# Attention in a two-block transformer kernel: probabilities times V for two blocks of queries in one pass

## The chip, the cores and the metric

The kernel runs on one core of a Trainium2 chip. The metric is device time of one execution in microseconds (us); before the change three runs gave a median of 1279.34 us (1277.62 to 1280.61). A difference of about 0.2% (2.6 us) is what a measurement of this kernel can tell from no change.

## What is computed

512 tokens of width 1024 pass through two blocks. The first holds two attentions of eight heads each (one latent, "MLA", with a causal mask by chunks of 64, one over a band of chunks with a table of relative biases), gates, a routed mixture of 32 experts and norms. The second holds an attention of 16 heads over three dilations (in the kernel one causal attention whose mask carries the three dilations) beside a state-space scan, and a layer norm. What the change touches is the same in all three attentions, cut to its core:

```python
sc = jnp.einsum('bqhd,bkhd->bhqk', qb, k).astype(jnp.float32) * scale
sc = jnp.where(mask[None, None], sc, NEG_INF)
p = jax.nn.softmax(sc, axis=-1).astype(v.dtype)
return jnp.einsum('bhqk,bkhd->bqhd', p, v)
```

## The kernel before, in words

All of this is one program whose order is written out by hand: each engine executes its instructions in the order in which the Python code issues them. TensorE works off two kinds of work, woven into each other: the attention's own short steps, and "fillers", long dense products (projections, 24 matmuls of 512 columns each per job) that stand in a queue of generators. `fill(ns)` issues fillers worth about so many nanoseconds of matmul; a debt is carried over, and a filler is issued in steps of 640 ns (three matmuls), 853 ns or 430 ns. When a filler job ends, it issues its evacuation (`fin_conv`, `scaled`, `fin_z`, `keep`, `fin_rope` and others) on VectorE and ScalarE; when the next one starts, its weights are split into a high and a low part (`whalf`: ScalarE writes `whi`, line 223, VectorE `wlo`, line 224).

`attention(units, filler, first)` (line 658) is called twice: for the first block with 32 units and 1700 ns of filler per step, for the second with 32 units and 5400 ns. A unit is one block of 128 queries (`i` from 0 to 3) of a pair of heads (`s` is 0 or 1); four units make a pair of heads, and block `i` sees keys 0 to 128(i+1). Step `idx` of the loop issues, in this order:

- the scores of unit `idx` into PSUM tiles `ps_sc` (line 680, or lines 235 to 237 as three products of split operands), then on VectorE the biased scores with their minimum (`st`, `mn`, line 683) and on ScalarE the exponentials with their sums (`p`, line 691);
- `fill(filler)`;
- the transposes of the probabilities of unit `idx-1` into `ps_tr` (line 703), and their copies into the tiles `pt`: of head 0 on ScalarE (line 708), of head 1 on VectorE (line 706);
- on VectorE, the division of unit `idx`'s probabilities by their sums (lines 715 and 716);
- the products with V for unit `idx-2` into `ps_o` (line 722): a product is 64 output rows by 128 queries, two heads side by side in the array, one such pair of products per block of keys. TensorE's trace shows two instructions for each 32-bit product and transpose, so 10 pairs of products of a pair of heads are 40 instructions.

So a unit's copies have a whole further step of filler before the products read them, and a unit's division has a step's filler before its transposes read it. The loop runs two steps past the last unit. `ps_o` has one buffer, `ps_sc` and `ps_tr` two, the tiles `pt` four.

Of the kernel before, what the change touches and what calls it, by code (L numbers as in the profile page):

```python
# [13 lines left out]
AF = mybir.ActivationFunctionType  # L14
# [4 lines left out]
P = 128  # L19
# [49 lines left out]
def tile_block(ctx: ExitStack, tc: tile.TileContext, xT, cols_d, rows_d, ln_d, consts_d, tabs_d, positions,  # L69
               w_ada, w1, v1, w_uq, w_ukv, rel, w_o, w_out, w_r, w_e, w2, v2, w_out2, out):  # L70
    nc = tc.nc
    pe, ve, se, ge = nc.tensor, nc.vector, nc.scalar, nc.gpsimd
# [9 lines left out]
    def big(name, dt=F32):  # L82
        return ap.tile([P, 512], dt, tag="a", name=name)
# [3 lines left out]
    def tmp(name, dt=F32):  # L87
        return tp.tile([P, 512], dt, tag=name, name=name, bufs=TEMPS[name])
# [3 lines left out]
    def bank(tag, dt=F32):  # L92
        return pp.tile([P, 512], dt, tag=tag, name="ps_" + tag, bufs=BANKS[tag])
# [60 lines left out]
    def step():  # L154

        if running[0] is None:
            if not queue:
                return 0
            job = queue.pop(0)
            job.start()  # L160
            if not job.wide:
                ahead()
            flush()
            running[0] = (job, job.gen())
        job, g = running[0]
        c = next(g, None)
        if c is None:
            job.done = True
            running[0] = None
            return 1  # L170
        return c
# [3 lines left out]
    def fill(ns):  # L175
        debt[0] += ns
        while debt[0] > 0:
            c = step()
            if c == 0:
                debt[0] = 0.0  # L180
                return
            debt[0] -= c
# [468 lines left out]
    for t in range(4):  # L651
        o = bank("d")
        sl = slice(t * P, (t + 1) * P)
        mm3(o, kv_h[0][:, sl], kv_l[0][:, sl], wv[0], wv[1], True, True)
        v = big("va")
# [2 lines left out]

    def attention(units, filler, first):
        n = len(units)  # L660
        for idx in range(n + 2):
            if idx < n:
                u = units[idx]
                for nxt in units[idx:idx + 2]:
                    nxt["need"]()
                if not idx:
                    fill(first)
                u["before"]()
                qs, ks, rsl, tab, scale = u["qk"]()
                i = u["i"]  # L670
                w = P * (i + 1)
                u["st"], u["mn"] = [], []
                for s in range(2):
                    sc = bank("sc")
                    sl = slice(i * P, (i + 1) * P)
                    if isinstance(qs[s], tuple):
                        (qh, ql), (kh, kl), wide = qs[s], ks[s], max(w, 256)
                        mm3(sc[:, :wide], qh[rsl[s], sl], ql[rsl[s], sl], kh[rsl[s], :wide], kl[rsl[s], :wide], True, True)
                    else:
                        pe.matmul(sc[:, :w], qs[s][rsl[s], sl], ks[s][rsl[s], :w], start=True, stop=True)  # L680
                    st = tmp("st")
                    mn = small([P, 1], "mn")
                    ve.tensor_tensor_reduce(st[:, :w], sc[:, :w], tab[s][:, 512 - w:], op0=OP.add, op1=OP.min,  # L683
                                            scale=-scale, scalar=3e38, accum_out=mn)
                    u["st"].append(st)
                    u["mn"].append(mn)
                u["p"], u["l"] = [], []
                for s in range(2):
                    pt = tmp("p")
                    l = small([P, 1], "l")  # L690
                    se.activation(pt[:, :w], u["st"][s][:, :w], AF.Exp, bias=u["mn"][s], scale=-1.0, accum_out=l)  # L691
                    u["p"].append(pt)
                    u["l"].append(l)
                u["mid"]()
            fill(filler)
            if 0 <= idx - 1 < n:
                u = units[idx - 1]
                w = P * (u["i"] + 1)
                u["t"] = []
                for s in range(2):  # L700
                    tr = bank("tr")
                    for j in range(u["i"] + 1):
                        pe.transpose(tr[:, j * P:(j + 1) * P], u["p"][s][:, j * P:(j + 1) * P], ident)  # L703
                    tt = tmp("pt")
                    if s:
                        ve.tensor_copy(tt[:, :w], tr[:, :w])
                    else:
                        se.activation(tt[:, :w], tr[:, :w], AF.Copy)
                    u["t"].append(tt)
            if idx < n:  # L710
                u = units[idx]
                w = P * (u["i"] + 1)
                for s in range(2):
                    rl = small([P, 1], "rl")
                    ve.reciprocal(rl, u["l"][s])
                    ve.tensor_scalar(u["p"][s][:, :w], u["p"][s][:, :w], rl, None, op0=OP.mult)  # L716
            if 0 <= idx - 2 < n:
                u = units[idx - 2]
                i, o, v, vc = u["i"], u["o"](), u["v"], u["vc"]
                for j in range(i + 1):  # L720
                    for s in range(2):
                        pe.matmul(o[64 * s:64 * s + 64, i * P:(i + 1) * P], v(j)[:, vc + 64 * s:vc + 64 * s + 64],
                                  u["t"][s][:, j * P:(j + 1) * P], start=j == 0, stop=j == i,
                                  tile_position=(0, 64 * s))
                u["after"](o)
                for key in ("st", "p", "t"):
                    u.pop(key)

    def pair_units(jobs, before, qk, v, vc, fin):
        o = {}  # L730
# [56 lines left out]
    units = []  # L787
# [47 lines left out]
    x1, xr, u = [], [], []  # L835
# [17 lines left out]
    st = {}  # L853
# [49 lines left out]
    for m in range(KC):  # L903
        t = big("x1")
# [51 lines left out]
    u = None  # L956
# [75 lines left out]
    for t in range(5):  # L1032
        ts_ = range(4) if t == 4 else range(t + 1)
        for t2 in ts_:
            pe.matmul(rk[:, t * NE:(t + 1) * NE], trib if t2 == t else oneb, Ab[:, t2, :], start=t2 == 0,
                      stop=t2 == ts_[-1])
# [185 lines left out]
    o = bank("tr")  # L1222
# [102 lines left out]
    for gi, group in enumerate(GROUPS):  # L1325
# [5 lines left out]
        for b, n in enumerate(group):  # L1331
# [31 lines left out]
            pt, csh = slots_back([w[:, b * P:(b + 1) * P] for w in pw])  # L1363
# [18 lines left out]
    for m in range(8):  # L1382
        o = opened[m] if m < len(opened) else combine_open(outs[:-1], pts[:-1], m)
# [25 lines left out]
    with tc.For_i(0, nblk, 1):  # L1409
# [5 lines left out]
        for i in range(6):  # L1415
            for h in range(2):
                t = big("wo")
# [6 lines left out]
        for t in range(4):  # L1424
            s = slice(t * CAP, (t + 1) * CAP)
            ve.tensor_scalar(po_[:, s], iota, kb_[:, t:t + 1], None, op0=OP.is_equal)
            ve.tensor_scalar(pw_[:, s], po_[:, s].bitcast(F32), wb_[:, t:t + 1], None, op0=OP.mult)
        o = bank("d")
        for d in range(KC):
            for t in range(4):  # L1430
                g = 2 * t + d // 4
                s = slice((d % 4) * P, (d % 4 + 1) * P)
# [6 lines left out]
        o = bank("tr")  # L1439
        for t in range(4):  # L1440
            pe.transpose(o[:CAP, t * P:(t + 1) * P], pw_[:, t * CAP:(t + 1) * CAP], ident)
        pt, cs, junk = big("pt_", F32R), small([P, 1], "cs"), tmp("st")
# [5 lines left out]
        for k in range(KC):  # L1448
            pe.matmul(gu[:CAP], xo[:, k * CAP:(k + 1) * CAP], we[k],
                      start=k == 0, stop=k == KC - 1, tile_position=(0, 0))  # L1450
# [3 lines left out]
        for h in range(2):  # L1454
            o = bank("sc")
            for q in range(2):
                pe.matmul(o[:CAP], ht[:, q * P:q * P + CAP], we[8 + 2 * q + h], start=q == 0,
                          stop=q == 1, tile_position=(0, 0))
# [8 lines left out]
    o = bank("o")  # L1467
    for k in range(KC):
        j = k % 4
# [3 lines left out]
    for k in range(KC):  # L1473
# [8 lines left out]
        else:  # L1482
            t = tmp("sq")
# [233 lines left out]
    units = []  # L1717
    for p in range(NP):
        us = pair_units(lambda p=p: [jq[p], jk[p]], lambda p=p: load_tab(p), lambda p=p: ([q2[p]] * 2, [k2_[p]] * 2, half, tab2[p], 0.125),
                        lambda j, p=p: vt[4 * (p // 4) + j], (p % 4) * P, fin_att(p))  # L1720
# [148 lines left out]
    for t in range(4):  # L1869
        n = 1 if t < 3 else 2  # L1870
        for i in range(n):
            o = bank(("sc", "sc", "tr", "o")[t] if not i else "d")
            c = slice(i * 512 // n, (i + 1) * 512 // n)
# [7 lines left out]
        v, rr = small([P, 1], "lnv"), small([P, 1], "lnr")  # L1881
        ve.tensor_scalar(v, mv[:, 1:2], 1e-5, None, op0=OP.add)
        ge.tensor_tensor(rr, v, mhalf[:, 0:1], op=OP.pow)
        for b in range(2):
            u = x2t[t, b]
            ve.scalar_tensor_tensor(u, u, mv[:, 0:1], lnb[b], op0=OP.subtract, op1=OP.mult)
        for b in range(2):
            u = x2t[t, b]
# [123 lines left out]
```

## Time and profile before

| what | us |
|---|---|
| median of three runs | 1279.34 |
| the profiled execution | 1281.25 |
| its span, first to last instruction | 1279.3 |
| TensorE matmul busy | 1213.9 (95%) |
| VectorE busy | 740.4 (58%) |
| ScalarE busy | 459.0 (36%) |
| GpSimd busy | 271.0 (21%) |

The profiled execution's time and its span are those of the same execution. The share of TensorE is high over the whole span; the granted TensorE clock is 0.9 of full speed or more in each of the 40 slices of the span. In the rows below PE is TensorE, PEld its weight loads, DVE VectorE, ACT ScalarE, POOL GpSimd.

### The profile page before, as it was taken

The page shows a single profiled execution, that of the slowest core. Times are in us where ns is not written, and L with a number is a line of the kernel's source. Part 1 is how long each engine was busy: PE and PEld are TensorE (multiplying, and loading weights), DVE is VectorE, ACT ScalarE, POOL GpSimd, SP SyncE. Part 2 cuts the span into 40 slices and gives each one's busy share as a digit, 9 for nine tenths or more (in the row PEclk, how much of TensorE's full clock was granted, in tenths as well). Part 3 has the DMA queues.
Part 4 walks back from the last instruction along what each step waited for, and adds up shares of the span by engine and source line. Part 5 has one row for each costly group of instructions (what it writes and reads, how often), then busy time and mean ns, then how long its engine had stood idle before and what let it go on. Part 6 is the DMA issues. An engine that isn't in the chain of part 4 may idle for free. (4 is left out here: it accounts for less than half of the span.)

```text
span 1279.3 us, 18709 instructions
## 1 busy us (share of the span) xinstructions
PE 1213.9 (95%) x6746; PEld 854.1 (67%) x6746; DVE 740.4 (58%) x1566; ACT 459.0 (36%) x1011; POOL 271.0 (21%) x232
## 2 busy tenths in 40 slices
PE   7999999999999799999998899999999999899997
PEld 4676676788887555444442477777777777666776
DVE  6856777534434633332322472677878776777766
ACT  4344554423324422121211153444444444354330
POOL 4333221000020200000100050424232330343321
PEclk9999999999999899999999999999999999999999
DMA  9624345032264656899999733222221212112321
GB/s 353 243 85 149 129 135 187 29 114 91 93 221 156 219 198 243 317 390 388 386 357 396 291 99 99 68 81 69 78 70 50 83 67 73 43 34 86 113 66 66
DMA packets 77966, 205.13 MB, mean 160 GB/s; under 512 B 9424, under 2 KB 9552, under 8 KB 77872
## 3 DMA queue, kind: packets, MB, share of 16 engines
q1 hardware_dynamic: 75840, 197.66, 43.4%
q0 software_dynamic: 1888, 6.18, 1.5%
q8 instruction: 54, 0.88, 0.3%
q14 instruction: 40, 0.33, 0.1%
q10 hardware_dynamic: 144, 0.09, 0.1%
HBM read 201.79 MB, written 2.10 MB: 159 GB/s over the span
## 5 line engine op out<-in xcount | busy, mean ns | idle before, releaser
L224 DVE TENSOR_TENSOR wlo<-w,whi 128x512 fp32r<-128x512 f32 x200 | 157.2, 825 | 113.9 <-ACT whi L223 101.5
L235 PE MATMUL ps_d<-x2h,whi 128*128 128x512 f32 x352 | 143.1, 406 | 0.0
L237 PE MATMUL ps_d<-x2h,wlo 128*128 128x512 f32 x352 | 138.6, 394 | 0.0
L236 PE MATMUL ps_d<-x2l,whi 128*128 128x512 f32 x352 | 138.5, 393 | 0.0
L223 ACT ACTIVATE whi<-w 128x512 fp32r<-128x512 f32 x200 | 115.3, 620 | 37.8 <-PE ps_d L236 16.4
L691 ACT ACTIVATE p<-st,mn 128x128 f32<-128x128 f32 (+3 forms) x128 | 71.0, 555 | 147.6 <-DVE mn L683 147.6
L1302 PE MATMUL ps_o<-we,xg 128*32 128x512 f32 (+1 forms) x592 | 111.0, 600 | 3.1 <-DMA we<-in_w_e_dram 2.8
L235 PEld LDWEIGHTS ps_d<-x2h,whi 128*128 128x128 f32 x352 | 66.9, 190 | 20.5 <-issue 5.3
L235 PE MATMUL ps_d<-h1h,whi 128*128 128x512 f32 x192 | 78.4, 409 | 0.0
L237 PEld LDWEIGHTS ps_d<-x2h,wlo 128*128 128x128 f32 x352 | 66.8, 190 | 15.2 <-DVE wlo L224 0.7
L236 PEld LDWEIGHTS ps_d<-x2l,whi 128*128 128x128 f32 x352 | 66.8, 190 | 12.6
L237 PE MATMUL ps_d<-h1h,wlo 128*128 128x512 f32 x192 | 75.0, 390 | 0.0
L236 PE MATMUL ps_d<-h1l,whi 128*128 128x512 f32 x192 | 74.9, 390 | 0.0
L1302 PEld LDWEIGHTS ps_o<-we,xg 128*32 128x32 f32 (+1 forms) x592 | 26.5, 117 | 67.0 <-issue 40.2
L1145 ACT ACTIVATE xg<-ps_d,mods 128x256 f32<-128x256 f32 (+1 forms) x48 | 21.4, 489 | 108.8 <-PE ps_d L1141 108.8
L716 DVE TENSOR_SCALAR p<-p,rl 128x128 f32<-128x128 f32 (+3 forms) x128 | 57.2, 447 | 4.5
L1140 PE MATMUL ps_d<-ph,gh 128*128 128x256 f32 (+1 forms) x192 | 54.0, 311 | 1.2 <-DVE ph L1114 1.2
L208 DVE TENSOR_TENSOR eol<-ps_sc,eoh 128x512 fp32r<-128x512 f32 x26 | 17.9, 691 | 59.6 <-ACT eoh L205 59.6
L1141 PE MATMUL ps_d<-ph,gl 128*128 128x256 f32 (+1 forms) x192 | 52.0, 300 | 0.0
L1124 POOL TENSOR_TENSOR pw<-ph,route 128x256 f32<-128x256 f32 (+1 forms) x24 | 17.2, 746 | 162.7 <-PE ps_o L1302 95.2
L1317 PE MATMUL ps_sc<-wd,p 128*32 128x512 f32 (+1 forms) x272 | 47.6, 597 | 1.1 <-ACT p L1173 1.1
L703 PEld LDWEIGHTS ps_tr<-cst,p 128*128 128x128 f32 x320 | 38.0, 140 | 14.4 <-issue 4.2
(637 smaller groups left out, 2722.2 us busy)
## 6 DMA issues: line engine op xcount, KB each, us to landing
we<-in_w_e_dram SPq DMA_DIRECT2D x108, 512.0 KB, 7.0
w<-in_w_dram SPq DMA_DIRECT2D x68, 512.0 KB, 3.3
wd<-in_w_e_dram SPq DMA_DIRECT2D x104, 256.0 KB, 6.2
wa<-in_w_ada_dram SPq DMA_DIRECT2D x32, 512.0 KB, 5.5
w<-in_w_out_dram SPq DMA_DIRECT2D x32, 512.0 KB, 3.4
wa<-in_w_ada_dram SPq DMA_DIRECT2D x32, 256.0 KB, 5.4
w<-in_v_dram SPq DMA_DIRECT2D x12, 512.0 KB, 7.7
tab<-in_w_e_dram SPq DMA_DIRECT2D x24, 256.0 KB, 6.7
```

The lines of the kernel that those rows point to most:

```text
L223: se.activation(hi, raw[:, s], AF.Copy)
L224: ve.tensor_tensor(lo, raw[:, s], hi.bitcast(F32), op=OP.subtract)
L235: pe.matmul(o, lh, rh, start=first, stop=False)
L236: pe.matmul(o, lh, rl, start=False, stop=False)
L237: pe.matmul(o, ll, rh, start=False, stop=last)
L691: se.activation(pt[:, :w], u["st"][s][:, :w], AF.Exp, bias=u["mn"][s], scale=-1.0, accum_out=l)
L703: pe.transpose(tr[:, j * P:(j + 1) * P], u["p"][s][:, j * P:(j + 1) * P], ident)
L716: ve.tensor_scalar(u["p"][s][:, :w], u["p"][s][:, :w], rl, None, op0=OP.mult)
L1140: pe.matmul(o[:, q * w:(q + 1) * w], gh[g][:, s], ph[t], start=t == 0, stop=False)
L1141: pe.matmul(o[:, q * w:(q + 1) * w], gl[g][:, s], ph[t], start=False, stop=t == 3)
L1302: pe.matmul(gu[a:a + m, :], xg[k][:, b * P + a:b * P + a + m], ws[n, s, i][k % 2], start=k == 0, stop=k == KC - 1, tile_position=(0, a))
L1317: pe.matmul(o[a:a + m, :], ht[:, kk * P + a:kk * P + a + m], ws[n, s, 4 + kk, h], start=kk == 0, stop=kk == 1, tile_position=(0, a))
```

## The change

Two neighbouring units (`i` even, then odd) share the tiles of turned probabilities. For each head and each pair of key blocks there is one tile of 512 columns; the even unit's turned probabilities go into columns 0 to 127 and 256 to 383, the odd unit's into those beside them. A copy of a unit is therefore cut into pieces of one or two key blocks. The products with V are issued only in the steps in which an odd unit is transposed (`two`), for both units at once: 256 queries wide where both see the key block, 128 wide for the last one. They come in the same step as the odd unit's transposes, not in the one after: in such a step the filler is split, `filler - 1400` before the transposes and 1400 between the transposes and the products. The loop is one step shorter, so one `fill(filler)` less is called in each attention; those fillers are issued later.

```diff
@@ -658,7 +658,7 @@
 
     def attention(units, filler, first):
         n = len(units)
-        for idx in range(n + 2):
+        for idx in range(n + 1):
             if idx < n:
                 u = units[idx]
                 for nxt in units[idx:idx + 2]:
@@ -692,21 +692,29 @@
                     u["p"].append(pt)
                     u["l"].append(l)
                 u["mid"]()
-            fill(filler)
+            two = 0 <= idx - 1 < n and units[idx - 1]["i"] % 2
+            fill(filler - 1400 if two else filler)
             if 0 <= idx - 1 < n:
                 u = units[idx - 1]
-                w = P * (u["i"] + 1)
-                u["t"] = []
+                i = u["i"]
+                if i % 2 == 0:
+                    u["t"] = [[tmp("pt") for _ in range(1 + i // 2)] for s in range(2)]
                 for s in range(2):
                     tr = bank("tr")
-                    for j in range(u["i"] + 1):
+                    for j in range(i + 1):
                         pe.transpose(tr[:, j * P:(j + 1) * P], u["p"][s][:, j * P:(j + 1) * P], ident)
-                    tt = tmp("pt")
-                    if s:
-                        ve.tensor_copy(tt[:, :w], tr[:, :w])
-                    else:
-                        se.activation(tt[:, :w], tr[:, :w], AF.Copy)
-                    u["t"].append(tt)
+                    for h, tt in enumerate((u if i % 2 == 0 else units[idx - 2])["t"][s]):
+                        n_ = min(2, i + 1 - 2 * h)
+                        src = tr[:, 2 * h * P:(2 * h + n_) * P]
+                        if n_ == 2 and (2 * h + 1 < i or i % 2 == 0):
+                            dst = tt.rearrange("p (j i q) -> p j i q", j=2, i=2)[:, :, i % 2, :]
+                            src = src.rearrange("p (j q) -> p j q", j=2)
+                        else:
+                            dst = tt[:, (i % 2) * P:(i % 2 + n_) * P]
+                        if s:
+                            ve.tensor_copy(dst, src)
+                        else:
+                            se.activation(dst, src, AF.Copy)
             if idx < n:
                 u = units[idx]
                 w = P * (u["i"] + 1)
@@ -714,17 +722,21 @@
                     rl = small([P, 1], "rl")
                     ve.reciprocal(rl, u["l"][s])
                     ve.tensor_scalar(u["p"][s][:, :w], u["p"][s][:, :w], rl, None, op0=OP.mult)
-            if 0 <= idx - 2 < n:
-                u = units[idx - 2]
+
+            if two:
+                u, u0 = units[idx - 1], units[idx - 2]
+                fill(1400)
                 i, o, v, vc = u["i"], u["o"](), u["v"], u["vc"]
                 for j in range(i + 1):
+                    a, c = max(i - 1, j), (j % 2) * 256
                     for s in range(2):
-                        pe.matmul(o[64 * s:64 * s + 64, i * P:(i + 1) * P], v(j)[:, vc + 64 * s:vc + 64 * s + 64],
-                                  u["t"][s][:, j * P:(j + 1) * P], start=j == 0, stop=j == i,
+                        pe.matmul(o[64 * s:64 * s + 64, a * P:(i + 1) * P], v(j)[:, vc + 64 * s:vc + 64 * s + 64],
+                                  u0["t"][s][j // 2][:, c:c + (i + 1 - a) * P], start=j == 0, stop=j == i,
                                   tile_position=(0, 64 * s))
                 u["after"](o)
-                for key in ("st", "p", "t"):
-                    u.pop(key)
+                for w_ in (u, u0):
+                    for key in ("st", "p", "t"):
+                        w_.pop(key, None)
 
     def pair_units(jobs, before, qk, v, vc, fin):
         o = {}
```

Two places show what moves. The first is TensorE in the first attention, at the third and fourth block of queries of the band attention's second pair of heads (`ps_tr`: transposes, `ps_o`: products with V, `ps_sc`: scores of the next pair, `ps_d`: filler). Before:

```order
L703 MATMUL ps_tr<-cst,p 128x128 x6
L722 MATMUL ps_o<-pt,vb 64x128 x4
L680 MATMUL ps_sc<-ka,qa 128x128 x2
L235 MATMUL ps_d<-h1h,whi 128x512
L236 MATMUL ps_d<-h1l,whi 128x512
L237 MATMUL ps_d<-h1h,wlo 128x512
...
L703 MATMUL ps_tr<-cst,p 128x128 x8
L722 MATMUL ps_o<-pt,vb 64x128 x6
L680 MATMUL ps_sc<-ka,qa 128x256 x2
```

and after the change:

```order
L705 MATMUL ps_tr<-cst,p 128x128 x6
L680 MATMUL ps_sc<-ka,qa 128x128 x2
L705 MATMUL ps_tr<-cst,p 128x128 x8
L235 MATMUL ps_d<-h1h,whi 128x512
L236 MATMUL ps_d<-h1l,whi 128x512
L237 MATMUL ps_d<-h1h,wlo 128x512
...
L733 MATMUL ps_o<-pt,vb 64x256 x6
L733 MATMUL ps_o<-pt,vb 64x128 x2
L680 MATMUL ps_sc<-ka,qa 128x256 x2
```

The filler that stood ahead of the last eight transposes (six matmuls) now stands behind them, the four products between the two groups of transposes are gone, and eight products for both blocks stand behind the filler. No row but the scores is left between the two groups of transposes.

The second place is VectorE in the second attention, at the fourth block of queries of the third pair of heads (`sq` and `xbc`: evacuation of a filler's result and its convolution, `wlo`: the next filler's weights, `pt`: the copy of turned probabilities that the products wait for). Before:

```order
L1521 TENSOR_TENSOR sq<-ps_d,r3b 128x512
L1527 SCALAR_TENSOR_TENSOR xbc<-sq,cols,xbc 128x509
L1527 SCALAR_TENSOR_TENSOR xbc<-sq,cols,xbc 128x510
L1527 SCALAR_TENSOR_TENSOR xbc<-sq,cols,xbc 128x511
L224 TENSOR_TENSOR wlo<-w,whi 128x512 x2
L1531 SCALAR_TENSOR_TENSOR xbc<-sq,xbc 128x512
L706 COPY pt<-ps_tr 128x512
L715 RECIPROCAL rl<-l 128x1
L716 TENSOR_SCALAR p<-p,rl 128x128
```

and after the change:

```order
L1533 TENSOR_TENSOR sq<-ps_d,r3b 128x512
L1539 SCALAR_TENSOR_TENSOR xbc<-sq,cols,xbc 128x509
L1539 SCALAR_TENSOR_TENSOR xbc<-sq,cols,xbc 128x510
L1539 SCALAR_TENSOR_TENSOR xbc<-sq,cols,xbc 128x511
L715 COPY pt<-ps_tr 128x2x128
L715 COPY pt<-ps_tr 128x256
L723 RECIPROCAL rl<-l 128x1
L724 TENSOR_SCALAR p<-p,rl 128x128
```

The copy is in two pieces; it still stands behind the evacuation of the filler that ends ahead of the transposes, while the next filler's weights now come later.

## Rows read from the trace of the kernel before

**Rows 1.** windows of both attentions: us, busy PE, PEld, DVE, ACT, POOL; clock, DMA.

```profile
112.00:254.00 142.00, 138.81 (x959) 96.67 (x957) 101.68 (x335) 69.32 (x195) 20.75 (x21) 1.00 0.37 125
813.00:1081.00 268.00, 265.27 (x1522) 209.14 (x1520) 205.54 (x485) 119.25 (x284) 77.21 (x58) 0.99 0.22 71
```

**Rows 2.** timeline, PE, second attention: start us, us, engine, line, operation [idle before].

```profile
846.82 0.38 PE L703 MATMUL ps_tr<-cst,p 128*128 128x128 f32 x2
847.13 1.10 PE L722 MATMUL ps_o<-pt,v 128*64 128x128 f32 x16
848.15 0.45 PE L235 MATMUL ps_sc<-qkh 64*128 64x384 f32 x2
...
848.88 0.50 PE L235 MATMUL ps_d<-x2h,whi 128*128 128x512 f32 x1
```

**Rows 3.** timeline, PE, second attention, a step of a fourth block.

```profile
904.71 0.39 PE L235 MATMUL ps_d<-x2h,whi 128*128 128x512 f32 x1
...
906.07 1.04 PE L703 MATMUL ps_tr<-cst,p 128*128 128x128 f32 x8
907.04 0.88 PE L722 MATMUL ps_o<-pt,v 128*64 128x128 f32 x12
907.84 0.39 PE L235 MATMUL ps_sc<-qkh 64*128 64x256 f32 x2
```

**Rows 4.** timeline, PE, first attention, between third and fourth block.

```profile
172.21 0.66 PE L722 MATMUL ps_o<-pt,vb 128*64 128x128 f32 x8
172.80 0.71 PE L680 MATMUL ps_sc<-ka,qa 128*128 128x128 f32 x4
173.26 0.48 PE L235 MATMUL ps_d<-h1h,whi 128*128 128x512 f32 x1
...
174.73 1.04 PE L703 MATMUL ps_tr<-cst,p 128*128 128x128 f32 x8
```

**Rows 5.** timeline, DVE, first attention, the same stretch.

```profile
172.35 0.55 DVE L706 COPY pt<-ps_tr 128x384 f32<-128x384 f32 x1
...
173.01 0.49 DVE L716 TENSOR_SCALAR p<-p,rl 128x512 f32<-128x512 f32 x1
...
173.60 0.49 DVE L716 TENSOR_SCALAR p<-p,rl 128x512 f32<-128x512 f32 x1
```

**Rows 6.** timeline, DVE, first attention, the same after a first block.

```profile
164.03 0.29 DVE L706 COPY pt<-ps_tr 128x128 f32<-128x128 f32 x1 [0.30 <-PE ps_tr L703]
...
164.88 0.35 DVE L716 TENSOR_SCALAR p<-p,rl 128x256 f32<-128x256 f32 x1
```

**Rows 7.** waits of DVE for transposes: us in total, times, longest us.

```profile
DVE pt L706 <- PE ps_tr L703: 14.8, 14, 2.0
```

**Rows 8.** timeline, DVE, first attention, step of a second block.

```profile
133.50 0.55 DVE L683 CUSTOM_DVE_ANT_0 st<-ps_sc,tab 128x384 f32<-128x384 f32 x1
```

**Rows 9.** timeline, ACT, that step.

```profile
134.77 0.60 ACT L691 ACTIVATE p<-st,mn 128x384 f32<-128x384 f32 x1
...
135.37 0.36 ACT L708 ACTIVATE pt<-ps_tr 128x256 f32<-128x256 f32 x1
```

**Rows 10.** timeline, DVE, second attention, around the step of rows 3.

```profile
904.91 0.69 DVE L1521 TENSOR_TENSOR sq<-ps_d,r3b 128x512 f32<-128x512 f32 x1 [1.19 <-PE ps_d L237]
906.49 2.32 DVE L1527 SCALAR_TENSOR_TENSOR xbc<-sq,cols,xbc 128x509 f32<-128x509 f32 x3 [0.89 <-ACT xbc L1524]
...
910.53 0.68 DVE L706 COPY pt<-ps_tr 128x512 f32<-128x512 f32 x1
```

**Rows 11.** timeline, DVE, second attention, a filler of queries ends ahead of a second block.

```profile
996.97 0.69 DVE L1543 TENSOR_TENSOR sq<-ps_d,r3b 128x512 f32<-128x512 f32 x1
...
1000.77 0.41 DVE L706 COPY pt<-ps_tr 128x256 f32<-128x256 f32 x1
```

**Rows 12.** timeline, PE, that step.

```profile
995.46 0.44 PE L722 MATMUL ps_o<-pt,v 128*64 128x128 f32 x4
```

**Rows 13.** weight loads of the products, by line: ns min/median/max, first and last start.

```profile
L722 PEld LDWEIGHTS ps_o<-pt,v x320: 132/137/137, 820.2 to 1087.0; 128*64 128x64 f32 x160
```

## The prediction, made before the result was known

> **What bounds the kernel now.** I read the shares of the engines first, then the windows of the two attentions, then the timelines of TensorE, VectorE and ScalarE around a step of each. TensorE is what runs out in both attentions: it is busy 138.8 of 142.0 us in the first and 265.3 of 268.0 in the second at a granted clock of 0.99 to 1.00, VectorE only 101.7 and 205.5 [rows 1]. So matmul time saved there shortens the kernel one for one, and each stop of TensorE lengthens it one for one; nothing behind it makes it up, since all fillers and the next scores stand behind a waiting instruction on its queue. Second reading: how late the helpers are. VectorE's copy of the turned probabilities waited for TensorE at only 14 of 64 places [rows 7]; at the other 50 VectorE was still busy with older work when the transposes were done. That lateness costs nothing now, since the products come a whole step of filler later. The reader is to see in the timelines how long the chains behind one step are, because the change takes that cover away.
>
> **What it saves on TensorE.** Per pair of heads 20 products become 12, but the columns that stream through stay the same: 20 of 128, then 8 of 256 and 4 of 128. A burst of 16 instructions takes 1.02 us to the next start [rows 2], one of 12 takes 0.80 [rows 3]: 0.055 us per instruction of 128 columns, and 0.14 us per burst that does not depend on its length. The burst of 8 agrees (0.59, of it 0.44 for the eight) [rows 4]. The columns' share therefore stays (an instruction of 256 I put at 0.11), and of 64 bursts 32 go: 32 x 0.145 = **4.6 us saved**. The split filler makes new borders between filler and products; filler next to transposes runs on without a gap, so I charge nothing for these, at most the whole 4.6. The step that the loop loses costs nothing: its filler is run later at the same price.
>
> **What it adds beside TensorE.** ScalarE and VectorE get 32 more copies each. A copy of 384 columns takes 0.55 us, of 256 0.41, of 128 0.29 [rows 5, 6, 11]; in two pieces 0.15 us more. Both engines have room [rows 1], but the 0.15 lies inside the chains below. Buffers, GpSimd's tables and the loads on SP's queue keep their places.
>
> **Wait 1: transposes of odd blocks, first attention.** Of the 1700 ns of filler only 300 stand ahead of them, and the order shows none there in 12 of 16 steps. So the scores alone lie between the even and the odd block's transposes, and in that time VectorE must copy, divide head 0 and divide head 1. For a fourth block: transposes end at 172.21, the division of head 1 at 174.09, 1.88 us later, and 2.03 with the copy in two pieces [rows 4, 5]. The scores take 0.46 [rows 4], four of the eight transposes 0.48 [rows 3]: TensorE has 0.94 us of work until it needs head 1, and waits 1.1. For a second block the chain is 1.2 us from the start of the copy [rows 6], plus the 0.1 until that starts; band scores take 0.73 [rows 2] and two transposes 0.22: wait 0.4; the MLA scores are longer (0.1). Four band steps x 0.4, four MLA x 0.1; fourth blocks: three x 1.1, the last one without scores 1.6, three with three filler matmuls ahead 0.25 each, one covered. Sum 1.6 + 0.4 + 3.3 + 1.6 + 0.75 = **7.6 us**. This takes VectorE as free when the transposes end; with half a microsecond of lateness at each of the 16 places it would be 8 more, which I keep for the upper end.
>
> **Wait 2: products behind ScalarE, first attention.** ScalarE's copy of head 0 stands behind both exponentials of the next unit. From the start of that unit's biased scores to the end of the copy it is 2.23 us [rows 8, 9]. VectorE starts these when it has divided head 1, so beside it TensorE has two transposes (0.22) and 1400 ns of filler, six matmuls or 1.36 us [rows 3]: a wait of 0.6. Six of the eight second blocks have no more filler than that, fourth blocks have shorter scores to wait for: 6 x 0.55 = **3.3 us**.
>
> **Wait 3: products in the second attention.** Here 4000 ns stand ahead of the transposes, which covers the division. But the products follow 1.36 us after the transposes, and the copy stands on VectorE behind the evacuation of whichever filler job has ended just before. The order shows such an end within six matmuls ahead of the odd transposes in 10 of 16 steps:
> - A convolved job ends right there, twice. It ends at 904.71, its three convolution steps at 908.81, two copies of 0.41 later it is 909.63 [rows 3, 10, 11]; the products are due 0.97 + 1.36 us after 904.71, at 907.04. Wait 2.6, twice 5.2.
> - A convolved job ends three matmuls (0.68) earlier and the next job's weights are split ahead of the copy, once: 910.53 - 904.71 + 0.82 = 6.64 against 3.01: 3.6.
> - A job of queries or keys ends three matmuls ahead, three times: from its evacuation to the end of the copy 4.21 [rows 11], with 0.2 ahead 4.4, against 0.68 + 0.53 + 1.36 = 2.57: 1.8 each. In one of them the state-space decays stand in between and the copy ends 5.7 us behind the place where the products will be due (1001.18 against 995.46) [rows 11, 12]; I take 5. Together 8.6.
> - A job of queries or keys ends right at the transposes, twice (1 each, an estimate, as only its evacuation is ahead), and the gates' jobs (1 for one, 0 for the other): 3.
>
> Sum 5.2 + 3.6 + 8.6 + 3 = **20.4 us**. The other six steps have their filler's end behind the copy: nothing.
>
> **The sum.** 7.6 + 3.3 + 20.4 - 4.6 = +26.7 us on the profiled execution's 1281.25: 1308. That execution lies 1.9 us over the median of the three runs, 1279.34, so the forecast in their terms is **1306 us**, 2.1% slower.
>
> **Rivals.**
> - *VectorE catches up.* Each stop gives VectorE and ScalarE time in which TensorE issues nothing new, so that chains behind earlier lateness shorten. For it: most of the 50 late places are backlog, not one chain. Against: in the convolved case VectorE idled 1.19 us for TensorE before it began [rows 10], so that chain is latency, not backlog. If half of all waits goes: 15.7 - 4.6 = +11, 1290 us. Chance 0.18.
> - *It is faster: weight loads pace the products.* Each product has a weight load of 132 to 137 ns [rows 13], longer than the 55 ns of an instruction. If these set the pace, 256 fewer would bring back 256 x 0.137 = 35 us, more than the waits: 31.3 - 4.6 - 35 = -8, 1271 us. It decides if a load costs over 0.10 us of TensorE's time. Against: 16 instructions in 1.02 us leave 0.064 us for each, less than half a load, so loads run beside the matmuls. Chance 0.04. The Trainium skill ("TensorE: Matmul & The Clock Gate", section "Back-to-back issue gap") says that weight load and matmul together set the pace, 81 ns at 128 columns and 131 at 512. By it, as an estimate with about 98 ns at 256, 640 x 81 ns would become 256 x 98 + 128 x 81, 16 us saved and a sum of +15; the trace's 55 ns disagree with it here.
> - *Most waits are hidden after all*, because a stop in one step leaves room for the next: within 0.2% of 1279 or a little faster or slower. That needs the waits to fall from 31 to under 8. Chance 0.06.
> - *Lateness adds up* (8 more in wait 1 and some in wait 3): above 1318. Chance 0.06.
> - That the change doesn't do what it says is ruled out by the order of its instructions.
>
> **How the numbers follow.** The forecast (1297 to 1318) has 0.66. The range 1287 to 1318 adds the catching-up case and leaves out the rest. About 0.2%, 2.6 us, is what a measurement tells from no change: faster 0.06 (weight loads 0.04, hidden waits 0.02), same 0.03, slower 0.91.
>
> **What would show it.** In the profile after: products' busy time about as before in columns, with 384 instructions, 256 of them wider; new waits of TensorE's transposes for VectorE's division in the first attention (near 8 us), of its products for VectorE's and ScalarE's copies in the second (near 20 us), single ones of 2 to 5 us; TensorE's busy share in both windows lower, all other stages as long as before. I am wrong if the products' waits are small although the copies stand behind the evacuations, or if 256 columns stream in much less than 0.11 us per instruction.

## The result and the profile after

The changed kernel takes 1317.3 us (median; 1315.07 to 1318.35), before it 1279.97: **slower by 2.9%**, ratio 1.0288 (95% interval 1.027 to 1.0306). The forecast was 1306 us within 1287 to 1318: the direction and the mechanism held, the size was 11 us short. The profiled execution took 1318.05 us. Its page begins:

```profile
span 1316.1 us, 18204 instructions
## 1 busy us (share of the span) xinstructions
PE 1220.8 (93%) x6490; PEld 846.8 (64%) x6490; DVE 744.0 (57%) x1598; ACT 462.3 (35%) x1043; POOL 269.7 (20%) x232
```

Before, TensorE had 6746 instructions, VectorE 1566 and ScalarE 1011: TensorE has 256 fewer and the two others 32 more each, as the change says. But TensorE's busy time did not fall, it rose from 1213.9 to 1220.8 us. The windows of the two attentions (the columns are those of [rows 1]; from the first transpose to the first instruction behind the attention):

```profile
114.70:266.00 151.30, 136.86 (x826) 88.89 (x824) 101.96 (x346) 69.68 (x207) 19.97 (x20) 1.00 0.34 116
825.30:1118.70 293.40, 274.18 (x1407) 208.29 (x1405) 207.29 (x501) 120.52 (x299) 77.06 (x58) 0.97 0.20 65
```

The same stretches of before:

```profile
112.80:252.90 140.10, 137.31 (x954) 95.82 (x952) 100.58 (x330) 68.10 (x191) 20.75 (x20) 1.00 0.37 124
813.10:1087.30 274.20, 271.48 (x1560) 214.07 (x1558) 207.94 (x489) 120.42 (x286) 77.21 (x58) 0.99 0.22 70
```

The first attention became 11.2 us longer, the second 19.2, although 24 filler matmuls (at 0.23 us, 5.5 us) left the second one and are run behind it: 24.7 us in truth. TensorE stands idle 14.4 us in the first stretch (2.8 before) and 19.2 in the second (2.7 before). In the second the granted clock is also lower, 0.97 against 0.99. VectorE's and ScalarE's busy times are as before. What TensorE waited for, first stretch, then second (engine, line and what it waited for: us in total, times, longest):

```profile
PE ps_tr L705 <- DVE rl L723: 10.1, 12, 2.3
PE ps_o L733 <- ACT pt L717: 2.7, 6, 1.2
...
PE ps_o L733 <- DVE pt L715: 0.2, 1, 0.2
```

```profile
PE ps_o L733 <- ACT pt L717: 13.1, 7, 3.9
PE ps_o L733 <- DVE pt L715: 6.0, 7, 1.5
```

These are the three waits of the prediction: transposes for the division (10.1 us), products for copies in the first attention (2.9), products for copies in the second (19.1). In the trace of before the first stands with 1.4 us at two places, the others not at all:

```profile
PE ps_tr L703 <- DVE p L716: 0.8, 1, 0.8
PE ps_tr L703 <- DVE rl L715: 0.6, 1, 0.6
```

**Wait 1 in the rows.** VectorE, first attention, between the third and fourth block of a pair of the band attention:

```profile
180.68 0.62 DVE L715 COPY pt<-ps_tr 128x256 f32<-128x256 f32 x2 [1.66 <-PE ps_tr L705]
...
181.41 0.49 DVE L724 TENSOR_SCALAR p<-p,rl 128x512 f32<-128x512 f32 x1
...
182.00 0.49 DVE L724 TENSOR_SCALAR p<-p,rl 128x512 f32<-128x512 f32 x1
```

and TensorE beside it:

```profile
179.77 0.87 PE L705 MATMUL ps_tr<-cst,p 128*128 128x128 f32 x6
180.48 0.61 PE L680 MATMUL ps_sc<-ka,qa 128*128 128x128 f32 x4
182.04 1.22 PE L705 MATMUL ps_tr<-cst,p 128*128 128x128 f32 x8 [0.95 <-DVE rl L723]
```

VectorE was free (it idled 1.66 us for these transposes), and the chain of copy, division, division ends 1.81 us after it starts, while TensorE had only the scores to run. The transposes start when head 0 is divided (181.90), after 0.95 us of visible waiting; those of head 1 wait for their division inside the same row, which takes 1.22 us in place of 1.04 [rows 3], 0.18 more. Together that is the case that the prediction worked out, at 1.1 us. The longest wait, 2.3 us, stands at a second block that was put at 0.4: there a split of a filler's weights, on ScalarE and then VectorE, stood ahead of the copy, a lateness that the prediction kept for its upper end.

**Wait 3 in the rows.** The longest one; TensorE has run nine filler matmuls behind the transposes and stands (1026.98 is the second head):

```profile
1025.59 0.95 PE L733 MATMUL ps_o<-pt,v 128*64 128x256 f32 x2 [3.89 <-ACT pt L717]
1026.98 1.54 PE L733 MATMUL ps_o<-pt,v 128*64 128x256 f32 x6 [0.43 <-DVE pt L715]
1028.45 0.80 PE L235 MATMUL ps_d<-x2h,whi 128*128 128x512 f32 x1
```

ScalarE and VectorE meanwhile, all engines in one view:

```profile
1021.51 1.19 DVE L1665 TENSOR_TENSOR csd<-ps_d,csd 32x128 fp32r<-32x128 f32 x4 [1.90 <-ACT csd L1662]
1022.73 0.69 DVE L1555 TENSOR_TENSOR sq<-ps_d,r3b 128x512 f32<-128x512 f32 x1
1023.46 0.63 ACT L205 ACTIVATE qkh<-sq 128x512 fp32r<-128x512 f32 x1 [1.98 <-DVE sq L1555]
1024.00 1.13 ACT L223 ACTIVATE whi<-w 128x512 fp32r<-128x512 f32 x2
...
1024.64 1.95 DVE L224 TENSOR_TENSOR wlo<-w,whi 128x512 fp32r<-128x512 f32 x2 [1.22 <-ACT whi L223]
1025.15 0.38 ACT L717 ACTIVATE pt<-ps_tr 128x256 f32<-128x256 f32 x1
...
1026.51 0.41 DVE L715 COPY pt<-ps_tr 128x256 f32<-128x256 f32 x1
```

The state-space decays, the evacuation of the filler and the split of the next filler's weights stand ahead of both copies. The prediction argued from VectorE's copy; ScalarE's has the same queue ahead of it, and its line is named for more of the waiting because it is needed first.

**What was not forecast: the clock.** TensorE behind this stop:

```profile
1029.47 0.63 PE L237 MATMUL ps_d<-x2h,wlo 128*128 128x512 f32 x1
1029.89 0.63 PE L235 MATMUL ps_d<-x2h,whi 128*128 128x512 f32 x1
...
1032.77 0.40 PE L236 MATMUL ps_d<-x2l,whi 128*128 128x512 f32 x1
1033.00 0.40 PE L237 MATMUL ps_d<-x2h,wlo 128*128 128x512 f32 x1
```

Matmuls of 512 columns begin 0.43 us apart, then 0.23: the lower of the two clock levels (1.2 GHz), until 1032.5. The second attention has four stretches at this level (the columns are those of [rows 1]):

```profile
943.90:947.30 3.40, 3.40 (x11) 2.39 (x9) 0.63 (x3) 0.00 (x0) 0.00 (x0) 0.50 0.48 159
984.80:988.20 3.40, 3.40 (x10) 2.50 (x9) 3.33 (x9) 1.43 (x4) 3.23 (x3) 0.51 0.28 92
1005.30:1008.70 3.40, 3.40 (x17) 2.27 (x14) 1.79 (x8) 0.55 (x3) 1.04 (x1) 0.50 0.21 84
1025.80:1032.60 6.80, 6.37 (x18) 4.04 (x17) 2.10 (x7) 0.00 (x0) 0.00 (x0) 0.50 0.22 77
```

Just ahead of each TensorE had stood 2 to 4 us for its products. It is busy for 16.6 us in them; with 0.20 us lost of each 0.43 that is some 7.7 us, an estimate. Before had one such stretch in this attention (from 971, 3.4 us, some 1.6 us lost). Over the whole span before had others: the fourteenth of the 40 slices of its page shows a clock of 0.8, not 0.9 or more.

**Waits inside a row.** Not all waiting shows as idle time, since the ends of matmuls are modelled. A fourth block's products, at a clock of 1.00:

```profile
922.74 0.65 PE L733 MATMUL ps_o<-pt,v 128*64 128x256 f32 x2
924.89 1.73 PE L733 MATMUL ps_o<-pt,v 128*64 128x256 f32 x14 [1.50 <-DVE pt L715]
```

The first two instructions take 2.15 us to the next start; four times 128 columns take 0.22 where nothing waits. So 1.9 us are lost, and 1.50 is shown.

### The profile page after: what moved, and what is told of

Read it like the earlier page. It is cut to its first block, busy times and chain, and to the rows that moved or that the text cites. A ratio compares the mean times of both kernels' runs of the same rounds, so it can differ in the third digit from the quotient of the medians.

```text
span 1316.1 us, 18204 instructions
## 1 busy us (share of the span) xinstructions
PE 1220.8 (93%) x6490; PEld 846.8 (64%) x6490; DVE 744.0 (57%) x1598; ACT 462.3 (35%) x1043; POOL 269.7 (20%) x232
## 5 line engine op out<-in xcount | busy, mean ns | idle before, releaser
L235 PE MATMUL ps_d<-x2h,whi 128*128 128x512 f32 x352 | 146.3, 416 | 0.0
L1157 ACT ACTIVATE xg<-ps_d,mods 128x256 f32<-128x256 f32 (+1 forms) x48 | 21.4, 488 | 107.0 <-PE ps_d L1153 107.0
L705 PE MATMUL ps_tr<-cst,p 128*128 128x128 f32 x320 | 48.7, 276 | 10.3 <-DVE rl L723 10.1
```

Of the source, the lines that this page charges most:

```text
L235: pe.matmul(o, lh, rh, start=first, stop=False)
```

## The experiments

All are compared with the kernel before, run on the same chip (1280 to 1281 us). Experiments 2 and 5 edit the kernel before, the others the change. Line numbers in the rows are each kernel's own.

**1. The widening alone.** The products go one step later, so that their cover comes back:

```diff
-        for idx in range(n + 1):
+        for idx in range(n + 2):
...
-            two = 0 <= idx - 1 < n and units[idx - 1]["i"] % 2
-            fill(filler - 1400 if two else filler)
+            two = 0 <= idx - 2 and units[idx - 2]["i"] % 2
+            fill(filler)
+            if two:
+                u, u0 = units[idx - 2], units[idx - 3]
+                i, o, v, vc = u["i"], u["o"](), u["v"], u["vc"]
+                for j in range(i + 1):
...
```

> The widening alone: products of both blocks in one burst as in the change, same shared tiles and split copies, but a whole step later, behind an undivided filler, so that every copy has a step of filler ahead of its reader, as before. Theory 1 (the loss is the lost cover: waits of TensorE for the division and the copies, and the clock that falls in them): all waits go, about 1.6 and 2.7 us idle in the two attentions as before, and 32 fewer bursts at 0.145 us remain: 1280 - 4.6 = 1275 us, near 1277 if the spared borders come back elsewhere. Rival 2 (the wide form itself costs: two-piece copies load VectorE and ScalarE, 256-column products run slower per column): slower than before, 1285 us or more, and the larger part of the 37 us is found here. Rival 3 (bursts have no cost of their own, the 0.14 us is only another border): 1280 us, no change.

Measured: 1280.36 us, ratio 0.9999 (0.9987 to 1.001). The waits for copies are gone, and of those for the division one of 1.0 us is left, at a place where before waits 1.4; so the widening doesn't cost. But the 4.6 us aren't saved in time either: rival 3 has the number, and the interval leaves at most 1.7 us of a saving. TensorE in the second attention:

```profile
841.87 0.39 PE L237 MATMUL ps_d<-x2h,wlo 128*128 128x512 f32 x1
842.19 1.73 PE L703 MATMUL ps_o<-pt,v 128*64 128x256 f32 x16
843.85 0.44 PE L714 MATMUL ps_tr<-cst,p 128*128 128x128 f32 x2
844.22 0.45 PE L235 MATMUL ps_sc<-qkh 64*128 64x384 f32 x2
```

The row of products holds 12 instructions of 256 columns and 4 of 128, 28 times 128 columns. It takes 1.66 us to the next start: 0.14 + 28 x 0.054. So columns cost what they did, and a burst still has its 0.14. But a burst of products isn't the only work with a border. The filler matmul ahead of the products takes 0.32 us to the next start where one ahead of filler takes 0.23, 0.09 more at each burst. And the last instruction of a burst of transposes takes 0.20 us to the scores and 0.11 to another transpose, 0.09 more; before, it took the same 0.20 to the products (0.31 for two in [rows 2]), so this border isn't new, it stays when the products go. Above the pace within bursts, two steps had 2 x (0.09 + 0.15) = 0.48 us before and have 0.09 + 0.15 + 2 x 0.09 = 0.42 here: an estimate of some 2 us less over 32 pairs of steps. The windows of the two attentions agree in sign:

```profile
112.90:251.40 138.50, 135.30 (x826) 91.55 (x824) 99.11 (x347) 68.56 (x207) 20.21 (x20) 1.00 0.37 125
809.40:1083.70 274.30, 270.17 (x1431) 208.60 (x1429) 207.19 (x505) 121.61 (x302) 76.73 (x58) 0.99 0.22 71
```

TensorE is busy 3.3 us less than before and idle 1.8 us more, in small waits.

**2. The move alone.** From before: own tiles, one copy a head, 128 columns, but the place of the change:

```diff
-        for idx in range(n + 2):
+        for idx in range(n + 1):
...
-            fill(filler)
+            two = 0 <= idx - 1 < n and units[idx - 1]["i"] % 2
+            fill(filler - 1400 if two else filler)
...
-            if 0 <= idx - 2 < n:
-                u = units[idx - 2]
+            for u in units[idx - 2:idx] if two else []:
+                if u["i"] % 2 == 0:
+                    fill(1400)
```

> The move alone: tiles, copies and products as before (one copy a head, 20 products of 128 columns for each pair of heads), but the products of both blocks stand in the step of the odd block's transposes behind 1400 ns of filler, as in the change, and the loop is one step shorter. Theory 1: the whole loss comes with the move: 1312 to 1320 us, idle of TensorE near 13 us in the first and 19 us in the second attention; somewhat less than the change's, if the second piece of a copy (0.15 us at each place) lies in the waits. Rival 2 (wide form costs): within 5 us of before. The weight-load rival of the prediction (137 ns for each product): 256 more products than the change, 35 us more than it, 1350 us.

Measured: 1315.03 us, ratio 1.0261 (1.0236 to 1.0286), against 1.0288 (1.027 to 1.0306) for the change. The move makes nearly the whole loss, and the waits are the same ones; second attention:

```profile
PE ps_o L724 <- ACT pt L709: 10.7, 7, 3.5
PE ps_o L724 <- DVE pt L707: 7.0, 7, 1.3
```

17.7 us in place of 19.1. The change itself is 2.3 us slower still; with these runs 7 us apart that doesn't price the copies in two pieces. With 256 instructions more it isn't slower than the change: weight loads don't pace the products.

**3. More filler between transposes and products**, second attention:

```diff
-            fill(filler - 1400 if two else filler)
+            fill(filler - part if two else filler)
...
-                fill(1400)
+                fill(part)
...
-    attention(units, 5400, 1300)
+    attention(units, 5400, 1300, 2800)
```

> The change with 2800 instead of 1400 ns of filler between transposes and products, in the second attention alone. Theory 1: each of the nine places where the products wait there (2.32, 0.77, 1.50, 2.31, 2.09, 2.55, 4.32, 1.50, 1.79 us of gaps) gets 1.36 us more cover, 19.2 us of idle fall to about 7.5, and with one or two of three falls of the clock gone as well: 1303 to 1306 us. Rival (the copies are late because the engines of the copies are short of time altogether, so that cover only moves the wait): 1314 to 1318 us.

Measured: 1302.63 us, ratio 1.0175 (1.0154 to 1.0196), just under the expected 1303 to 1306, but not by the expected rows. The waits of the second attention:

```profile
PE ps_tr L705 <- DVE rl L723: 8.6, 8, 3.6
```

No product waits for a copy any more (7.5 us were expected to stay). Instead the transposes wait for the division, with 2600 ns ahead of them in place of 4000. The two covers come out of the same step's filler: what one wait gains, the other partly takes.

**4. The first attention late** as in experiment 1, the second as in the change; `attention_late` is the function of experiment 1:

```diff
-    attention(units, 1700, 2600)
+    attention_late(units, 1700, 2600)
```

> First attention with the late wide products, second attention as in the change. Theory 1: the first attention's part of the loss goes: it was 11.2 us longer than before, and gains up to 2.3 us by fewer bursts: 1317.3 - 11.2 to 13.5 = 1304 to 1306 us; the second attention keeps 19 us of idle. Rival (waits of the first attention are made up later, since its fillers are the same work): 1317 us.

Measured: 1307.37 us (1303.77 to 1312.36), ratio 1.0223 (1.0199 to 1.0247), 9.9 us under the change, less than the 11.2 to 13.5 expected, in runs that lie 8.6 us apart. The first attention is worth some 10 us, the second the other 27, and neither makes up for the other: the products of the second still wait 19.2 us.

**5. Narrow products, late and in one burst.** The products of before (128 columns, own tiles), placed as in experiment 1:

```diff
             fill(filler)
+            both = units[idx - 3:idx - 1] if idx - 2 >= 0 and units[idx - 2]["i"] % 2 else []
+            for u in both:
+                i, o, v, vc = u["i"], u["o"](), u["v"], u["vc"]
+                for j in range(i + 1):
...
```

> Products as before (128 columns, own tiles, one copy a head), but those of both blocks in one burst, at the place of the first experiment: a whole step late, behind an undivided filler and ahead of the next transposes. It differs from the first experiment in the width alone. Theory 1 (columns set the time, and what the merging of bursts spares comes back as a border between transposes and scores, which measured 0.20 us in the first experiment as the one between products and scores did before): same as the first experiment and as before, 1278 to 1282 us. Rival 2 (widening saves and merging costs, and the two cancelled in the first experiment): 1283 us or more. The weight-load rival of the prediction: 256 instructions more than the first experiment, up to 35 us slower than it.

Measured: 1280.79 us, ratio 1.0001 (0.9988 to 1.0014), the same as with 256 columns. The instructions of the second attention, first here, then in experiment 1 (durations min/median/max):

```profile
L701 PE MATMUL ps_o<-pt,v x320: 272/273/324, 830.8 to 1088.9; 128*64 128x128 f32 x160
```

```profile
L703 PE MATMUL ps_o<-pt,v x192: 272/379/431, 826.6 to 1083.6; 128*64 128x256 f32 x128, 128*64 128x128 f32 x64
```

320 or 192 instructions, the same time: neither the width of the products nor, in this order, their merging is worth anything that can be told.

**6. Splits behind the copies**, second attention. While an odd step's first part of filler is issued, the preparation of the next job is held back:

```diff
-            if not job.wide:
-                ahead()
-            flush()
+            if held:
+                held[0] = job
+            else:
+                if not job.wide:
+                    ahead()
+                flush()
...
+            if hold and two:
+                held.append(None)
...
+            if held:
+                job = held.pop()
+                if job:
+                    if not job.wide:
+                        ahead()
+                    flush()
```

> The change, but in the second attention the split of the next filler's weights and the late part of an evacuation (tanh and gate) are issued behind the copies of an odd block, where a filler job ends ahead of them. Theory 1 (the products wait since the copies stand behind such work on ScalarE's and VectorE's queues): the five places with splits ahead of the copy wait 2.32, 2.31, 2.55, 4.32 and 1.79 us, most of it goes, 8 to 11 us, the four others (0.77, 1.50, 2.09, 1.50 us) stay: 1306 to 1309 us. Rival (the evacuation itself and the chain of the scores set these waits, the splits only fill the time): 1314 to 1318 us.

Measured: 1301.84 us, ratio 1.0175 (1.0155 to 1.0195), 15.5 us under the change. Waits and window of the second attention:

```profile
PE ps_o L746 <- ACT pt L724: 7.4, 7, 3.3
PE ps_o L746 <- DVE pt L722: 3.8, 3, 1.5
```

```profile
823.50:1102.40 278.90, 266.55 (x1407) 203.41 (x1405) 207.35 (x501) 119.92 (x299) 76.85 (x58) 0.99 0.20 67
```

The waits fell by 7.9 us, at the low end of what was expected; the gain is twice that, and the time lies under the expected 1306 to 1309. TensorE is also busy 7.6 us less with the same 1407 instructions (266.6 against 274.2), at a granted clock of 0.99 in place of 0.97. One stretch at the lower level is left in the window (from 976.5) where the change has four. So the stops cost about as much again in the pace of the work between them.

**7. VectorE's chain shortened**, first attention:

```diff
-                        if s:
+                        if s and not (act and i % 2 == 0):
                             ve.tensor_copy(dst, src)
...
-    attention(units, 1700, 2600)
+    attention(units, 1700, 2600, True)
```

> The change, but in the first attention both copies of an even block are made by ScalarE, so that VectorE begins the division of the odd block's probabilities at once. Theory 1 (the transposes of odd blocks wait for the chain copy, division, division on VectorE): the chain is shorter by 0.7 us at a fourth block and 0.3 at a second one, and 10.2 us of idle ahead of and within the transposes fall to 4 to 6: 1311 to 1313 us. Rival (the exponentials or the biased scores ahead of the division end last): no change, 1315 to 1319 us.

Measured: 1311.41 us, ratio 1.0233 (1.0217 to 1.0249), 5.9 us under the change. Of the first attention's waits

```profile
PE ps_tr L705 <- DVE rl L723: 3.5, 4, 1.9
...
PE ps_tr L705 <- ACT pt L717: 1.1, 2, 0.7
```

and 0.3 us more are left where 10.1 stood: the chain copy, division, division sets wait 1.

**8. Fewer borders.** As experiment 1, with the products behind the transposes:

```diff
-    TEMPS = {"sq": 3, "st": 3, "p": 4, "pt": 4, "tab": 4, "bc": 1}
+    TEMPS = {"sq": 3, "st": 3, "p": 4, "pt": 6, "tab": 4, "bc": 1}
...
-                fill(1400)
```

> As the first experiment, but the products of both blocks stand behind the next transposes (filler, transposes, products, scores), with six buffers for the turned probabilities instead of four and two buffers of another pool fewer. Theory 1 (borders between kinds of work on TensorE cost, not bursts): two steps have borders of 0.10 + 0.15 (transposes to products, products to scores) and 0.09 (transposes to scores) above the pace within a burst, 0.34 us, against 0.48 before and 0.43 in the first experiment: 16 pairs of steps twice, 32 x 0.14 = 4.5 us below before, 1276 us; 3 us below the first experiment. Rival (borders cost the same at every place): 1280 us.

Measured: 1278.71 us, ratio 0.9989 (0.9979 to 0.9998): 1.4 us less than before, of the 4.5 expected. It is the fastest kernel of the study, by a margin under what the measurement can tell from no change. In its trace the last instruction of a burst of products takes 0.20 us to the scores, as before, and that of the transposes 0.20 to products or scores; all steps without products keep that border. Waits for the division come to 3.2 us in the two attentions, where before has 1.4. That these 1.8 us hide more of the saving is argued from the rows; no run shows it without them.

**9. The waits mended together**, experiments 6 and 7 with 2100 ns behind the transposes:

```diff
-    attention(units, 1700, 2600)
+    attention(units, 1700, 2600, act=True)
...
-    attention(units, 5400, 1300)
+    attention(units, 5400, 1300, part=2100, hold=True)
```

> The change with its waits mended together: both copies of an even block on ScalarE in the first attention (5.9 us gained alone), splits behind the copies of odd blocks in the second (15.5 us gained alone), and there 2100 instead of 1400 ns of filler behind the transposes. Theory 1 (the lost cover is the whole loss, and its causes add up): the eight places that still waited in the second attention with the splits behind (0.39, 0.77, 1.50, 0.39, 2.09, 0.82, 3.31, 1.50 us) get 0.68 us more cover, 4.9 us less, against 1 to 3 us of new waits for the division, since only 3300 ns stand ahead of the transposes: 1317.3 - 5.9 - 15.5 - 2 to 4 = 1292 to 1294 us. Rival (a wait that is mended in one place comes back in the next): 1298 us or more.

Measured: 1295.2 us (1292.53 to 1298.11), ratio 1.0126 (1.0094 to 1.0158), between the 1292 to 1294 expected and the rival's 1298. The gains of 6 and 7 alone, 5.9 and 15.5, explain 21.4 of the 22.1 us gained; the 700 ns more of cover bring nothing that can be told from the spread. Its waits over both attentions:

```profile
PE ps_tr L712 <- DVE rl L736: 6.6, 6, 2.1
...
PE ps_o L746 <- ACT pt L724: 5.8, 6, 2.6
```

The step's filler, shared between two chains, covers neither in full. 15 us of the loss remain.

## Why the prediction was right in direction and short in size

- **What bounds the kernel** held: TensorE's stops lengthened the kernel one for one and more, and neither attention made up for the other (experiment 4).
- **Saved 4.6 us: not shown as time, and its reason was incomplete.** "0.14 us per burst that does not depend on its length ... of 64 bursts 32 go" is right about the burst: where nothing waits, the change's bursts take 0.80 and 1.66 us, the same 0.14 and 0.054 per 128 columns. But it is a border between kinds of work, and its neighbours have borders too: transposes to products or scores 0.09, which stays, and filler to products 0.09, which the prediction charged at nothing with the whole 4.6 as its bound. In the change's order two steps have 0.09 + 0.09 + 0.15 = 0.33 us (transposes to scores, filler to products, products to scores; transposes ahead of filler have none) against 0.48, an estimate of 4.8 us saved. So the term may stand, with the new border made up by one that it didn't count. No run times it apart from the stops. In the orders that were timed without them the time fell by 0.4 us (experiment 1, 2 by its borders) and 1.4 us (experiment 8, 4.5 by its borders).
- **Wait 1, 7.6 us**: 10.1 visible at 12 places, and the transposes' rows take 2.1 us more than before (25.7 against 23.6 us of busy time). Mechanism shown by experiment 7; mis-sized by taking VectorE as free, at one second block above all (2.3 in place of 0.4).
- **Wait 2, 3.3 us**: 2.9 visible.
- **Wait 3, 20.4 us**: 19.1 us of visible waits, 17.7 and 19.2 in experiments 2 and 4. By place: the two convolved jobs 1.5 each (2.6 forecast), the one with splits 2.6 (3.6), the three jobs of queries or keys 2.3, 2.3 and 4.3 (1.8, 1.8 and 5), the two that end right at the transposes 0.8 and 2.1 (1 each), the gates 1.8 (1). Single places missed by up to 1.1 us and cancelled.
- **The moved filler** costs what it did, only later: the stretch behind the second attention is 5.4 us longer, 24 matmuls at 0.23.
- **What was left out: the price of a stop is more than its visible length.** Second attention, in truth 24.7 us longer: idle time explains 16.5, busy time 8.2. Some 6 of these are the lower clock (7.7 less the 1.6 of before, both estimates). The rest is waiting inside rows, less what the borders save, and the two aren't separated: the products take 27.3 us of busy time where experiment 1 spends 20.7 on the same instructions. The prediction's sum has no term for the clock; these 6 us are the larger part of the 11 that the forecast is short, the others, as far as the rows show, are waits that came out longer than they were sized. That the visible waits add up to nearly the 31.3 forecast (32.1) is in part luck, since those inside rows don't count in it.
- **Rivals.** VectorE did not catch up: waits have their full size. Weight loads are ruled out twice: 320 products and 192 take the same time (experiments 1, 5), and with 256 instructions more the move alone isn't slower than the change (experiment 2). By the Trainium skill ("TensorE: Matmul & The Clock Gate", section "Back-to-back issue gap") widening to 256 columns was an estimate of 16 us of gain; the runs show none.

## What to carry to other kernels

Before putting a consumer closer to its producer, list what stands ahead of the producer on its engine's queue at that place: helper engines that were busy for 57% and 35% of the span held TensorE up at 9 of 16 such steps of the second attention, since their work came in blocks of up to 5 us. Cover that two chains share is one sum; dividing it anew moves part of a wait to the other chain (experiment 3), issuing other work behind the urgent copy removes part of it outright (experiment 6). A fixed cost seen at the end of a burst is a border between two kinds of work: before calling it saved, add up all borders of the new order.

## What the runs showed of the hardware

- A burst of column-tiled products costs 0.14 us beside its columns; the last transpose takes 0.20 us to scores or products, 0.11 to the next transpose, and 0.03 to a filler matmul, whose own successor then starts 0.31 us later in place of 0.23. (Other than the section on the kernel says, a transpose is one instruction in the trace and only a product two: the two attentions of before have 320 transposes and 640 instructions for 320 products.)
- 128 or 256 columns per instruction: 0.054 to 0.055 us per 128 columns, with weight loads of 137 ns for each, hidden in both.
- The longest stop of the change, 3.89 us ahead of 1025.59, was followed by the lower clock level from 1025.8 to 1032.6. In experiment 6 the same place stopped for 3.31 us, and the window around it has a granted clock of 1.00:

```profile
1006.00:1024.00 18.00, 14.32 (x69) 10.45 (x68) 12.12 (x33) 8.31 (x21) 4.17 (x4) 1.00 0.18 60
```

In the change itself two places stopped for the same 1.43 and 0.9 us (834.02 and 942.04); only the second was followed by the lower level. So the length of one stop alone doesn't decide. What does was not tried.
